# Where the adaLN sums are computed: all blocks after the first four in mixer A, one in each slot, in a bank of the ring of three

## The chip, the core and the metric

The kernel runs on one core of a Trainium2 chip. The metric is the device time of one execution in microseconds (us), the median of several runs. TensorE (PE) multiplies, PEld is its weight load, VectorE (DVE), ScalarE (ACT) and GpSimd (POOL) do the rest, and SyncE's queue (SP) issues the DMAs.

## What is computed

Two layers of a diffusion trunk, each a token mixer (A: windowed attention, B: neighbourhood attention) followed by a gated ConvFFN, over 640 tokens (512 latent, 128 context) of width 1024. Every sub-layer is modulated by a shift, a scale and a gate that come from one small product per layer:

```python
def adaln(cond, w_ada, b_ada):
    m = jax.nn.silu(cond) @ w_ada + b_ada
    return [t[:, None, :] for t in jnp.split(m, 6, axis=-1)]
...
for i in range(DEPTH):
    mp = adaln(c_ctx[None, :], w_ada[i], b_ada[i])
    ms = adaln(c, w_ada[i], b_ada[i])
    hp = modulate(rmsnorm(xp, norm_attn_w[i]), mp[0], mp[1])
    hs = modulate(rmsnorm(xs, norm_attn_w[i]), ms[0], ms[1])
    ...                                   # attention: op, o_s
    xp = xp + mp[2] * op
    xs = xs + ms[2] * o_s
    hp = modulate(rmsnorm(xp, norm_ffn_w[i]), mp[3], mp[4])
    hs = modulate(rmsnorm(xs, norm_ffn_w[i]), ms[3], ms[4])
    xp = xp + mp[5] * conv_ffn(hp, ...)
    xs = xs + ms[5] * conv_ffn(hs, ...)
```

`w_ada[i]` is 1024 x 6144 in float32, 24 MB a layer. The condition has two rows (latent and context), so the product is tiny in columns but has to read all of `w_ada`.

## The kernel before

**Blocks of adaLN.** The 6144 columns of a layer are 12 blocks of 512. A block (l, n) comes in four DMAs of 512 KB (`ada_tile`, L169, ring `adst` of four tiles: exactly one block). It is made in two steps by the generator `ada_queue` (L191). Step one: `ada_sums` (L174), eight float32 products (16 matmul records) that put four partial sums into the four 32-row strips of one PSUM bank `ps_ada`; a copy of that bank to SBUF, `adrow` (L182, on ACT in mixer A, on DVE in the FFNs); and the DMAs of the next block's tiles, which reuse the tiles just summed. Step two: `ada_done` (L219). For a gate (n = 4, 5, 10, 11; there the row's bias comes by a small DMA) one product (2 records), a copy and a DMA to DRAM; for the other n four products (8 records) that fold the strips into columns and one DVE addition of the bias into `mcol` (L231). Blocks (0, 0) to (0, 3) are made at the start and don't concern us; 20 remain.

**Mixer A** is a loop of 21 slots (L1006). Slot n works on head group g = n // 5 and token block t = n % 5: it runs the QKV product of (g, t) (`Q`, eight steps of three matmuls each), places the keys and queries of the slot before (`T`: transposes into banks of the ring `p`), scores of the block three slots back (`S`) and the product with the values of the block four slots back (`V`: transposes into ring `p`, then `ps_o`). The order in which PE takes these steps is written out by hand in `SLOTS` (L30): "A0" to "A3" for slots 0 to 3, then "a0" to "a4" by t, and "AT" for the last slot, which also holds half of the output projection. PE keeps this program order (`k.chain`), and the DMAs that go through `dma` keep theirs up to slot 18 (`k.dma_chain`); the rest is ordered by the scheduler. PSUM rings here: `mm` (2 banks: the QKV sums), `p` (3), `s` (2), `o` (1). ACT splits every weight into a high part (`whi`, L158) and POOL (DVE in a few cases) makes the low part (`wlo`, L161); weights of the next group are loaded at the ends of slots with t = 0, 1 and 4 (L1041).

Six blocks, (0, 4) to (0, 9), are made in the slots 1, 3, 5, 8, 11 and 14 (`ADA_SLOTS`, L38): step one after the fourth entry of the slot's order, step two after the tenth, with `ps_ada` in the ring `mm`.

**The FFN** of a layer (`finish_layer`, L1142, and `ffn`, L913) makes 44 up-products of 48 matmuls (7.1 us each), a convolution on DVE, SiLU on ACT and, in six groups, the down-products. PE's order is the scheduler's here. After the up-products listed in `ADA_UPS` (L54) `after("up")` takes one step of the queue: the twelve blocks (0, 10), (0, 11), (1, 0) to (1, 9) in layer 0, the two blocks (1, 10), (1, 11) in layer 1, with `ps_ada` in the ring `dn`.

Of the kernel before, what the change touches and what calls it, by code (L numbers as in the profile page):

```python
# [29 lines left out]
SLOTS = {"A0": "QQQQQQQQTT", "A1": "QQQQQQQTQT", "A2": "QQQQQQQTQT", "A3": "QSQSQQQSQQQTTS",  # L30
         "AT": "SSVOOVVSVOSOOTVVOOSOVSTVVOSVSOOOVVSOVSOVVSSOVOOVOVOOOV",
         "a0": "VSQQSQVVSSVVTQQVTQQQQ", "a1": "QSSVVQQVSVSQQQQVTQVQT", "a2": "SQVQQSVSVSQQVVTQQQTVQ",
         "a3": "QQVSSQQVVVSVVSQQQQTTQ", "a4": "SSQQQVVSSVQQQVVQTVQTQ",
         "b0": "SVQQSQHPPVQQQQVQ", "b1": "VQHPSQQSHPQQVQQHV", "b2": "QHVQSPSQHQVQVQHPQ",
         "b3": "HHSQVSQHPQQQVQVHQP", "b4": "SHPQQVSVQQHQQVQPH",
         "BT": "OSPOPSSVOOSOPVVSSOHHPOHPVOOHPOPOHVOOHOOPHSOSVHHSVVPOHOSVHPSHPOOHPOHSSOPVSVSPOVSPOOOVPPOOPVVVOOV"}

ADA_SLOTS, ADA_PLACES = (1, 3, 5, 8, 11, 14), (4, 10)  # L38

START = "p p x0 p p x1 p p n0 x2 n1 p p x3 n2 p x4 n3 n4 p s f0 w0 w1 p p f1 f4 p f2 p p f3 q p w2 w3 p"  # L40

# [8 lines left out]
O_DVE = (), (0, 2)  # L50

LAST = "40a 41a 00a 01a 40b 41b 00b 01b 10 11 n4 20 n0 21 30 n1 31 n2 q6 n3"

ADA_UPS = (0, 1, 3, 4, 6, 7, 8, 9, 11, 12, 14, 15, 17, 18, 20, 21, 23, 24, 26, 27, 29, 30, 32, 33), (0, 1, 3, 4)  # L54

OPROJ = "00 10 20 01 11 21 n0 30 n1 40 w0 n2 31 41 w1 u0 n3d w2 u1 n4d u2 u0 u1 u2"

# [1 line left out]
def _f(ap):  # L59
    return ap.bitcast(F32)  # L60


class Trunk:
# [846 lines left out]
            nc.vector.scalar_tensor_tensor(z[:, a:b - 1], u[:, a + 1:b], w[:, 2:3], z[:, a:b - 1], op0=OP.mult, op1=OP.add)  # L910
        return z

    def ffn(self, l, hT, xs, groups, first, ahead, after):  # L913
        nc, fp = self.nc, self.fp
        gate = None
        f = 0
        for gi, n in enumerate(groups):
            gh = self.ap.tile([P, 4, T], F32R, name="gh", tag="act")
            gl = self.ap.tile([P, 4, T], F32R, name="gl", tag="act")
            for k in range(n):  # L920
                zz = []
                for ff in (f + k, f + k + NF):
                    if first:
                        u = first.pop(0)
                    else:
                        u = []
                        w = ahead.pop(0) if ahead else self.load_w(self.I["wup"][l, ff], 1024, self.wp)
                        for _ in self.up(hT, [w], u):
                            pass
                    zz.append(self.conv(u[0], ff, fp))  # L930
                    after("up")
                silu = nc.scalar.activation(zz[0], zz[0], AF.Silu)
                nc.vector.tensor_tensor(zz[0], zz[0], zz[1], OP.mult)
                nc.scalar.activation(gh[:, k], zz[0], AF.Copy)  # L934
                nc.gpsimd.tensor_tensor(gl[:, k], zz[0], _f(gh[:, k]), OP.subtract)  # L935
            last = gi == len(groups) - 1
            if last:
                self.pin_exp(silu)
            W = [self.load_w(self.I["wdown"][l, f + k], 1024, self.wp) for k in range(n)]
            f += n  # L940
            if gate is None:
                gate = self.load_gate(l, 1)
            if last:
                after("last", (gh, gl), W, gate)
                continue
            for t in range(NT):
                for _ in self.proj_part((gh, gl), W, xs, t, gate):
                    pass


def body(nc, tc, I, O):
    with ExitStack() as top:
        k = Trunk(nc, tc, I, O, top)
# [11 lines left out]
        hT = k.new_hT("hA")  # L965
        with ExitStack() as c1:
            sp = k.pool(c1, "start", side="right")
            xT = [k.ap.tile([P, 4, T], F32, name=f"xT{h}", tag="act") for h in range(2)]
            xt, W, sts = [], [], []
# [25 lines left out]
        with c2:  # L995
            k.mp = k.pool(c2, "mixa", side="right")
            k.qT_bufs, k.pexp_bufs = 3, 4
            k.a_setup(pin=True)
            k.first_post(xT, hT, 1, 2 * P, NS, nc.gpsimd, pin=True)
            k.first_post(xT, hT, 1, NS, T, nc.gpsimd, pin=True)  # L1000
            sts.append(k.a_begin(0))
            steps = k.ada_queue([(0, n) for n in range(4, 10)], True, "mm", 2)
            ofs, scs = [], {}
            k.xd = [k.dp.tile([NT, P, D], F32, name=f"xd{i}") for i in range(3)]
            place = iter(())
            for n in range(21):  # L1006
                g, t = n // 5, n % 5
                u = n - 4
                if t == 0 and 0 < g < 4:
                    sts.append(k.a_begin(g))  # L1010
                if n == 19:
                    k.dma_chain = False
                if n in (4, 14):
                    ofs.append(k.ap.tile([P, 4, T], F32, name="of", tag="act"))
                gens = {"T": place, "S": iter(()), "V": iter(()), "Q": iter(()), "A": steps}
                if 0 <= u + 1 < 20:
                    scs[u + 1] = []
                    gens["S"] = k.a_score(sts[(u + 1) // 5], (u + 1) // 5, (u + 1) % 5, scs[u + 1])
                if u >= 0:
                    gens["V"] = k.a_pv(sts[u // 5], u // 5, u % 5, scs[u], ofs[u // 10])  # L1020
                if g < 4:
                    place = iter(())
                    st = sts[g]
                    gens["Q"] = k.qkv(hT, W, t, lambda ps: k.a_post(st, g, t, ps)) if n else q0
                    place = k.a_place(st, t)
                    order = SLOTS[f"A{n}" if n < 4 else f"a{t}"]
                    if n in ADA_SLOTS:
                        a, b = ADA_PLACES
                        order = order[:a] + "A" + order[a:b] + "A" + order[b:]
                    run(gens, order)  # L1030
                else:
                    for v in (18, 19):
                        scs[v] = []
                    gens["S"] = chain(gens["S"], *(k.a_score(st, 3, v - 15, scs[v]) for v in (18, 19)))
                    gens["V"] = chain(gens["V"], *(k.a_pv(st, 3, v - 15, scs[v], ofs[1]) for v in (17, 18, 19)))
                    gens["O"] = k.o_first(0, "woa", ofs[0], xin, k.xd[0])
                    run(gens, SLOTS["AT"])
                if 5 <= n < 17:
                    k.b_scratch(2 * n - 10)
                    k.b_scratch(2 * n - 9)  # L1040
                if g < 3 and t in (0, 1, 4):  # L1041
                    Wn = k.load_group("wqa", g + 1, Wn if t else None, t)
                if t == 4 and g < 3:
                    W = Wn
            k.chain = False
            for _ in steps:
                pass
            k.ada_scale(0, 1)
        finish_layer(k, 0, "woa", ofs[1], k.xd[0], cw)
        adactx.close()  # L1050

# [3 lines left out]
def mixer_b(nc, k, tc, top, hT, W):  # L1055

        I = k.I
        with ExitStack() as c2:
# [34 lines left out]
            for s in range(41):  # L1093
# [32 lines left out]
                if t == 4:  # L1126
                    W = Wn
            k.chain = False
        finish_layer(k, 1, "wob", ofs[1], k.xd[2], cw)


def run(gens, order, only=""):

    for c in order:
        next(gens[c], None)
    for c, g in gens.items():
        if c not in only and c != "A":
            for _ in g:
                pass


def finish_layer(k, l, wo, of, xsrc, cw):  # L1142
    nc = k.nc
    with ExitStack() as c:
        k.xp = k.pool(c, f"x{l}", side="right")
        k.fp = k.pool(c, f"ffn{l}", side="right")
        if l == 1:
            k.adp = k.pool(c, "ada2", side="right")
        k.psf = ExitStack()
        k.psp = k.pool(k.psf, f"psf{l}", space=PSUM)  # L1150
        k.z_bufs = 4
# [6 lines left out]
        xs = []  # L1158
# [4 lines left out]
        hl = k.split_oT(of, l == 0)  # L1163
        W = k.load_o(wo, 1)
        hT = k.new_hT(f"hF{l}")
        k.ada_next = k.ada_tiles(l, 10)
        k.convc = k.fp.tile([P, 44, 4], F32, name="convc")
        nc.sync.dma_start(k.convc, k.I["conv"][l])
        k.chain = True
# [15 lines left out]
        first = [], [], []  # L1185
# [19 lines left out]
        ahead = []  # L1205
# [6 lines left out]
        k.wp = k.pool(c, f"wf{l}")  # L1212
        first = list(first)
        k.chain = False
        blocks = [(l, 10), (l, 11)] + [(1, n) for n in range(10) if l == 0]
        steps = k.ada_queue(blocks, False, "dn", 2)
        ups_done = iter(range(44))

        def after(kind, *args):
            if kind == "up":  # L1220
                if next(ups_done) in ADA_UPS[l]:
                    next(steps)
            else:
                last(*args)

        def last(g, W, gate):

            for _ in steps:
                pass
            if l == 0:  # L1230
                k.ada_scale(1, 0)
                k.ada_scale(1, 1)
# [35 lines left out]
            up = k.psp.tile([P, 2, 512], F32, name="ps_dn", tag="up", bufs=3)  # L1268
            for w in LAST.split():
# [4 lines left out]
                t, h = int(w[0]), int(w[1])  # L1274
# [4 lines left out]
                    done(t, h)  # L1279
            k.chain = False  # L1280

        k.ffn(l, hT, xs, (4, 4, 2, 4, 4, 4), first, ahead, after)
        if l == 1:
            k.psf.close()

# [75 lines left out]
```

## Time and profile before

| | us |
|---|---|
| median of 3 runs | 1744.81 (1744.4 to 1747.25) |
| the profiled execution, device time | 1744.18 |
| its span, first to last instruction | 1742.4 |
| PE busy | 1633.3 (94%) |
| PEld busy | 1457.8 (84%) |
| POOL, DVE, ACT busy | 951.9, 879.2, 762.1 |

The span divides into the start (to some 64 us), mixer A (to some 337), the end of layer 0's attention (to 389), FFN of layer 0 (to about 850), mixer B and its end (to about 1275) and FFN of layer 1. A busy PE is not PE at its peak: what counts is whether it waits, and how many matmuls stand in its queue. The granted clock of TensorE is a share of 2.4 GHz; it has two levels, 1.0 and 0.5 (1.2 GHz), and a number between is a mean over the stretch.

### The profile page before, as it was taken

To read this page: it belongs to the slowest core of one execution; us is meant where nothing else is said; L and a number is where in the kernel's file an instruction comes from. 1 tells how busy PE (TensorE), PEld (TensorE's weight loads), DVE (VectorE), ACT (ScalarE), POOL (GpSimd) and SP (SyncE) were. 2 spreads that over 40 slices of the span, in tenths; PEclk is the share of its full clock that TensorE was granted. 3 is DMA by queue.
4 is the path that set the end of the run, shared out by engine and by line. 5 is a ranking of instruction groups with operands and counts; after the bars stand their busy time and mean duration, and the time that the engine had idled before them with its cause. 6 is when DMAs were issued, how large, how long until landed. Compare 5 with 4: busy or idle time off the path is not lost.

```text
span 1742.4 us, 26277 instructions
## 1 busy us (share of the span) xinstructions
PE 1633.3 (94%) x9736; PEld 1457.8 (84%) x9736; DVE 879.2 (50%) x2136; ACT 762.1 (44%) x1696; POOL 951.9 (55%) x796
## 2 busy tenths in 40 slices
PE   5788988989999999999988999988999999999998
PEld 2577776878998879899878999987779999999997
DVE  4667767674333333242575667677753232432334
ACT  4366666354131322232356777775543222323231
POOL 1553555564464664556336777775455656746461
PEclk8999999999999999999989999999999999999999
DMA  8242232516252434321232211223522222213131
GB/s 348 95 126 82 100 106 96 175 65 217 85 194 97 139 130 143 109 100 61 73 101 81 60 52 49 71 93 118 201 98 97 80 78 74 84 61 97 49 97 61
DMA packets 73727, 184.85 MB, mean 106 GB/s; under 512 B 15080, under 2 KB 24808, under 8 KB 73600
## 3 DMA queue, kind: packets, MB, share of 16 engines
q1 hardware_dynamic: 73600, 183.18, 31.1%
q8 instruction: 77, 1.26, 0.3%
q14 instruction: 50, 0.41, 0.1%
HBM read 171.32 MB, written 14.12 MB: 106 GB/s over the span
## 4 chain that ended last, share of the span: by engine, by line
PE 80%; DVE 9%; ACT 4%; issue 3%; POOL 2%; DMA 2%; SPq 0%; POOLq 0%; DVEq 0%; ACTq 0%
PE ps_up L133 35%; PE ps_dn L133 19%; PE ps_mm L133 11%; PE ps_ada L133 3%; PE ps_o L133 2%; PE ps_op L133 2%; PE ps_s L133 2%; PE ps_p L139 2%; PE ps_tr L139 1%; DVE xT L262 1%; PE ps_row L133 1%; DMA wst<-in_wqa_dram 1%; PE ps_nt L139 1%; DVE xn L336 1%; DVE xtmp L459 1%
## 5 line engine op out<-in xcount | busy, mean ns | idle before, releaser
L133 PE MATMUL ps_up<-hF,whi 128*128 128x320 f32 x2688 | 600.9, 311 | 5.1 <-POOL hF L373 5.1
L161 POOL TENSOR_TENSOR wlo<-wst,whi 128x1024 fp32r<-128x1024 f32 (+3 forms) x192 | 419.4, 2190 | 231.9 <-ACT whi L158 200.8
L133 PEld LDWEIGHTS ps_up<-hF,whi 128*128 128x128 f32 x2688 | 453.6, 189 | 25.4 <-ACT z L907 6.7
L133 PE MATMUL ps_up<-hF,wlo 128*128 128x320 f32 x1344 | 415.7, 310 | 0.0
L158 ACT ACTIVATE whi<-wst 128x1024 fp32r<-128x1024 f32 (+3 forms) x195 | 186.5, 962 | 442.0 <-PE ps_dn L133 165.8
L133 PEld LDWEIGHTS ps_up<-hF,wlo 128*128 128x128 f32 x1344 | 252.9, 188 | 4.6 <-issue 2.6
L909 DVE SCALAR_TENSOR_TENSOR z<-ps_up,convc,z 128x511 f32<-128x511 f32 (+1 forms) x176 | 95.8, 544 | 283.2 <-ACT z L907 283.2
L460 POOL TENSOR_TENSOR x<-x,xtmp 128x512 f32<-128x512 f32 x100 | 129.6, 1301 | 148.5 <-DVE xtmp L459 148.2
L459 DVE TENSOR_TENSOR xtmp<-ps_dn,gate 128x512 f32<-128x512 f32 x120 | 81.8, 689 | 242.5 <-PE ps_dn L133 239.7
L133 PE MATMUL ps_mm<-whi,hB 128*128 128x384 f32 x580 | 181.3, 351 | 9.3 <-DVE rs_r L324 8.5
L133 PE MATMUL ps_dn<-whi,gh 128*128 128x512 f32 x440 | 172.9, 393 | 1.8 <-DVE xtmp L459 1.6
L133 PE MATMUL ps_dn<-wlo,gh 128*128 128x512 f32 x440 | 172.3, 392 | 0.0
L133 PE MATMUL ps_dn<-whi,gl 128*128 128x512 f32 x440 | 169.8, 389 | 0.0
L935 POOL TENSOR_TENSOR gl<-z,gh 128x640 fp32r<-128x640 f32 x44 | 69.2, 1572 | 90.3 <-ACT gh L934 90.3
L133 PEld LDWEIGHTS ps_mm<-whi,hB 128*128 128x128 f32 x580 | 108.7, 191 | 11.6 <-ACT vb L511 8.9
L133 PE MATMUL ps_mm<-whi,hA 128*128 128x384 f32 x320 | 101.2, 362 | 9.6 <-DVE hA L268 3.5
L907 ACT ACTIVATE z<-ps_up,convc 128x640 f32<-128x640 f32 x88 | 77.0, 875 | 68.6 <-PE ps_up L133 68.6
L910 DVE SCALAR_TENSOR_TENSOR z<-ps_up,convc,z 128x511 f32<-128x511 f32 (+1 forms) x176 | 96.6, 549 | 5.6
L133 PE MATMUL ps_mm<-wlo,hB 128*128 128x384 f32 x290 | 98.3, 339 | 0.0
L133 PEld LDWEIGHTS ps_dn<-whi,gh 128*128 128x128 f32 x440 | 82.6, 188 | 17.8 <-DVE xtmp L459 3.5
L133 PEld LDWEIGHTS ps_dn<-whi,gl 128*128 128x128 f32 x440 | 82.2, 188 | 17.1
L133 PEld LDWEIGHTS ps_dn<-wlo,gh 128*128 128x128 f32 x440 | 82.6, 188 | 13.7
(210 smaller groups left out, 2945.1 us busy)
## 6 DMA issues: line engine op xcount, KB each, us to landing
adst<-in_wada_dram SPq DMA_DIRECT2D x96, 512.0 KB
wst<-in_wup_dram SPq DMA_DIRECT2D x78, 512.0 KB
wst<-in_wdown_dram SPq DMA_DIRECT2D x44, 512.0 KB
wst<-in_wqb_dram SPq DMA_DIRECT2D x29, 384.0 KB
wst<-in_wqa_dram SPq DMA_DIRECT2D x16, 384.0 KB
xd<-xring SPq DMA_DIRECT2D x20, 256.0 KB
x<-xd SPq DMA_DIRECT2D x10, 512.0 KB
wst<-in_woa_dram SPq DMA_DIRECT2D x8, 384.0 KB
```

Of the source, the lines that this page charges most:

```text
L133: i = self.nc.tensor.matmul(out, lhsT, rhs, start=start, stop=stop)
L139: i = self.nc.tensor.transpose(out, in_, idn)
L158: i = nc.scalar.activation(hi, st, AF.Copy)
L161: (lo_eng or nc.gpsimd).tensor_tensor(lo, st, _f(hi), OP.subtract)
L262: i = nc.vector.tensor_scalar(v, v, A[:, j, f:f + 1], self.mcol[0][:, j, f:f + 1], op0=OP.mult, op1=OP.add)
L336: nc.vector.tensor_scalar(xn, x, self.rsqrt(ss, 1, D), None, op0=OP.mult)
L459: nc.vector.tensor_tensor(tmp, ps, gate[:, j, sl], OP.mult)
L460: (nc.gpsimd if pool_add else nc.vector).tensor_tensor(x[:, sl], x[:, sl], tmp, OP.add)
L907: nc.scalar.activation(z, u, AF.Identity, scale=w[:, 1:2], bias=w[:, 3:4])
L909: nc.vector.scalar_tensor_tensor(z[:, a + 1:b], u[:, a:b - 1], w[:, 0:1], z[:, a + 1:b], op0=OP.mult, op1=OP.add)
L910: nc.vector.scalar_tensor_tensor(z[:, a:b - 1], u[:, a + 1:b], w[:, 2:3], z[:, a:b - 1], op0=OP.mult, op1=OP.add)
L935: nc.gpsimd.tensor_tensor(gl[:, k], zz[0], _f(gh[:, k]), OP.subtract)
```

## The change

Every block after the first four is made in mixer A. The queue of steps now holds (0, 4) to (0, 11) and (1, 0) to (1, 11), 20 blocks; each of the slots 1 to 19 takes two steps, so one block; the twentieth, (1, 11), is made in the loop behind the slots that empties the queue. The places in a slot's order are now given for each kind of slot. `ps_ada` lies in the ring `p` of three banks instead of the ring `mm` of two. The FFNs make none: `after`, `ADA_UPS`, their queue, the early load of a block's tiles and the pool `ada2` of layer 1 go. What used the result of a block (`ada_scale`, `load_gate`) stays where it was.

```diff
-ADA_SLOTS, ADA_PLACES = (1, 3, 5, 8, 11, 14), (4, 10)
+ADA_PLACES = {"A1": (2, 4), "A2": (2, 4), "A3": (2, 4), "a0": (2, 6), "a1": (1, 3), "a2": (1, 4), "a3": (1, 4), "a4": (2, 4)}
-ADA_UPS = (0, 1, 3, 4, 6, 7, 8, 9, 11, 12, 14, 15, 17, 18, 20, 21, 23, 24, 26, 27, 29, 30, 32, 33), (0, 1, 3, 4)
...
                     zz.append(self.conv(u[0], ff, fp))
-                    after("up")
...
-            steps = k.ada_queue([(0, n) for n in range(4, 10)], True, "mm", 2)
+            steps = k.ada_queue([(0, n) for n in range(4, 12)] + [(1, n) for n in range(12)], True, "p", 3)
...
-                    order = SLOTS[f"A{n}" if n < 4 else f"a{t}"]
-                    if n in ADA_SLOTS:
-                        a, b = ADA_PLACES
+                    slot = f"A{n}" if n < 4 else f"a{t}"
+                    order = SLOTS[slot]
+                    if n > 0:
+                        a, b = ADA_PLACES[slot]
                         order = order[:a] + "A" + order[a:b] + "A" + order[b:]
...
-        if l == 1:
-            k.adp = k.pool(c, "ada2", side="right")
...
-        k.ada_next = k.ada_tiles(l, 10)
...
-        blocks = [(l, 10), (l, 11)] + [(1, n) for n in range(10) if l == 0]
-        steps = k.ada_queue(blocks, False, "dn", 2)
-        ups_done = iter(range(44))
-
-        def after(kind, *args):
-            if kind == "up":
-                if next(ups_done) in ADA_UPS[l]:
-                    next(steps)
-            else:
-                last(*args)
-
         def last(g, W, gate):
-            for _ in steps:
-                pass
...
-        k.ffn(l, hT, xs, (4, 4, 2, 4, 4, 4), first, ahead, after)
+        k.ffn(l, hT, xs, (4, 4, 2, 4, 4, 4), first, ahead, last)
```

## Rows read from the trace of the kernel before

**Rows 1.** The page's first part: busy time, share of the span, instructions.

```profile
PE 1633.3 (94%) x9736; PEld 1457.8 (84%) x9736; DVE 879.2 (50%) x2136; ACT 762.1 (44%) x1696; POOL 951.9 (55%) x796
```

**Rows 2.** Busy time by stage: length, PE, PEld, DVE, ACT, POOL; clock, DMA, GB/s.

```profile
103.60:162.00 58.40, 53.36 (x333) 44.59 (x331) 40.62 (x137) 40.13 (x115) 28.65 (x42) 1.00 0.35 104
...
222.80:282.10 59.30, 51.07 (x286) 43.95 (x284) 41.24 (x135) 43.23 (x120) 31.78 (x41) 0.94 0.21 65
...
389.00:850.00 461.00, 461.00 (x2838) 412.24 (x2838) 164.83 (x271) 134.37 (x152) 252.49 (x136) 1.00 0.36 125
1280.00:1313.00 33.00, 33.00 (x219) 27.65 (x218) 14.57 (x24) 13.53 (x15) 16.21 (x8) 1.00 0.46 160
```

**Rows 3.** The tile ps_ada, by form: count, ns min/median/max, first and last start.

```profile
L133 PE MATMUL ps_ada<-adst,cT x320: 589/592/617, 67.5 to 1302.3; 128*32 128x512 f32 x160
```

**Rows 4.** Timeline of PE around two blocks in layer 0's FFN: start, duration, instruction.

```profile
401.57 1.02 PE L133 MATMUL ps_ada<-adrow,sel 99*2 99x512 f32 x2
...
434.07 1.92 PE L133 MATMUL ps_ada<-adst,cT 128*32 128x512 f32 x16
435.92 0.56 PE L133 MATMUL ps_up<-hF,whi 128*128 128x320 f32 x2
...
443.06 0.95 PE L133 MATMUL ps_ada<-sel,adrow 98*128 98x2 f32 x8
443.87 0.48 PE L133 MATMUL ps_dn<-whi,gh 128*128 128x512 f32 x1
```

**Rows 5.** Busy time from one slot's squares (L559) to the next's, columns as above.

```profile
103.60:119.50 15.90, 14.27 (x92) 10.89 (x91) 9.21 (x29) 11.39 (x30) 8.93 (x12) 1.00 0.80 238
162.00:178.80 16.80, 13.79 (x69) 11.06 (x67) 9.61 (x28) 11.13 (x29) 9.17 (x12) 0.90 0.34 106
222.80:240.10 17.30, 14.08 (x67) 11.56 (x66) 9.68 (x28) 10.85 (x28) 8.73 (x11) 0.80 0.43 140
119.50:130.10 10.60, 9.39 (x60) 8.60 (x59) 8.08 (x27) 7.59 (x23) 6.75 (x8) 1.00 0.10 11
...
178.80:191.40 12.60, 11.99 (x83) 9.96 (x82) 8.32 (x28) 7.43 (x22) 4.68 (x6) 1.00 0.54 211
140.80:150.80 10.00, 9.94 (x70) 8.12 (x68) 6.99 (x25) 6.47 (x21) 2.35 (x4) 1.00 0.43 153
202.20:209.70 7.50, 7.28 (x47) 6.78 (x45) 6.54 (x23) 5.92 (x20) 2.34 (x4) 1.00 0.00 1
...
150.80:162.00 11.20, 9.88 (x61) 8.64 (x59) 8.43 (x29) 7.74 (x22) 5.85 (x10) 1.00 0.21 57
209.70:222.80 13.10, 12.59 (x84) 9.85 (x82) 9.11 (x32) 8.32 (x25) 6.53 (x11) 1.00 0.45 162
268.60:282.10 13.50, 10.49 (x62) 8.72 (x60) 9.37 (x29) 12.02 (x31) 10.12 (x12) 1.00 0.20 54
```

**Rows 6.** Timeline of PE in mixer A; in brackets, idle before and its releaser.

```profile
67.50 1.92 PE L133 MATMUL ps_ada<-adst,cT 128*32 128x512 f32 x16 [2.78 <-issue]
...
84.46 0.33 PE L133 MATMUL ps_mm<-wlo,hA 128*128 128x384 f32 x1
...
84.99 0.34 PE L133 MATMUL ps_mm<-wlo,hA 128*128 128x384 f32 x1
...
106.78 1.92 PE L133 MATMUL ps_ada<-adst,cT 128*32 128x512 f32 x16
...
171.94 0.44 PE L133 MATMUL ps_mm<-whi,hA 128*128 128x384 f32 x1 [1.04 <-ACT whi L158]
173.82 0.44 PE L133 MATMUL ps_mm<-wlo,hA 128*128 128x384 f32 x1 [1.44 <-POOL wlo L161]
```

**Rows 7.** Timeline of ACT: the copy of two blocks' sums in mixer A.

```profile
84.37 0.60 ACT L186 ACTIVATE adrow<-ps_ada 98x512 f32<-98x512 f32 x1 [0.21 <-PE ps_ada L133]
...
110.76 0.57 ACT L186 ACTIVATE adrow<-ps_ada 98x512 f32<-98x512 f32 x1
```

**Rows 8.** The stretch in which slot 5's tiles come in, columns as in rows 2.

```profile
108.50:121.00 12.50, 11.41 (x74) 10.08 (x71) 6.07 (x17) 9.68 (x23) 9.07 (x10) 1.00 0.97 278
```

More of the change, by code (lines that the diff above doesn't have):

```diff
@@ L911, in conv, with ffn @@
         return z
-    def ffn(self, l, hT, xs, groups, first, ahead, after):
+    def ffn(self, l, hT, xs, groups, first, ahead, end):
         nc, fp = self.nc, self.fp
@@ L935, in ffn @@
                 nc.gpsimd.tensor_tensor(gl[:, k], zz[0], _f(gh[:, k]), OP.subtract)
-            last = gi == len(groups) - 1
-            if last:
+            if gi == len(groups) - 1:
                 self.pin_exp(silu)
@@ L942, in ffn @@
                 gate = self.load_gate(l, 1)
-            if last:
-                after("last", (gh, gl), W, gate)
+            if gi == len(groups) - 1:
+                end((gh, gl), W, gate)
                 continue
```

## The prediction

> **What bounds the kernel now.** I read four views, in this order. First the page's busy shares: PE is busy for 94% of the span and no other engine for more than 55% [rows 1], so the question for every stage is whether PE waits there. Second, the busy time by stage. In the FFN of layer 0 PE is busy for all of its 461 us, and so it is in the part of layer 1's FFN that holds the two blocks; in mixer A it idles for 5.0 of 58.4 us in one head group and 8.2 of 59.3 us in another [rows 2]. Matmul time that leaves the FFNs is therefore worth its full length, and the same time put into mixer A can partly lie in waits that are there anyway. Third, mixer A slot by slot: the distance from one slot's squares (they end its QKV) to the next's, for slots of the same kind with a block in them and without [rows 5]. That is the price of a block in a slot, measured by the kernel itself. Fourth, single rows: what a block costs PE [rows 4], where PE waits in mixer A [rows 6], when the copy of the sums runs [rows 7], how long the tiles take to come [rows 8].
>
> **What leaves the FFNs.** 320 records of sums are 20 blocks of 16 [rows 3]; 14 of them stand in the FFNs. In an FFN the sums of a block start at 434.07 and the next up-product at 435.92: 1.85 us. Its second part takes 443.87 - 443.06 = 0.81 us, or, for a gate, by a record of 1.02 us that overlaps its follower a little, about 0.95 [rows 4]. Eight blocks of 2.66 and six gates ((0, 10), (0, 11), (1, 4), (1, 5), (1, 10), (1, 11)) of 2.80 are 21.3 + 16.8 = 38.1 us. PE never waits around them [rows 2, 4], so nothing covers this time: all 38.1 us come off. The copies on DVE and the tiles' DMAs that go with them lie beside PE and cost nothing now; they free nothing either, since DVE is busy for 165 of 461 us there. After the change the next engine in the FFN is POOL with 252 of then some 430 us, so PE stays the bound.
>
> **What is added to mixer A.** Thirteen more slots get a block, and one block stands behind the slots.
> - Kind a0 (slots 10 and 15). Slot 5, with a block, took 15.9 us; slots 10 and 15, without, took 16.8 and 17.3 [rows 5]. The block is *shorter than nothing* there, because a0 begins a head group and its QKV waits for weights (1.04 us for the high part, 1.44 for the low, in slot 10) [rows 6], and the granted clock in these two stretches falls to a mean of 0.90 and 0.80, against 1.00 in slot 5, where the block's matmuls stand where the wait was. I take -0.9 and -1.4: -2.3. Bounds: -1.4 to +2.8 each. By the Trainium skill (TensorE: Matmul & The Clock Gate, Part 1: The HAM clock gate) TensorE is throttled to half its clock when it idles and released by activity; slots 5, 10 and 15 agree.
> - Kind a1 (slots 6, 16): slot 11 with a block 12.6, slot 6 without 10.6: +2.0 each, 4.0.
> - Kind a3 (13, 18): slot 8 with a block 10.0, slot 13 without 7.5: +2.5 each, 5.0.
> - Kind a4 (4, 9, 19): slot 14 with a block 13.1, slot 9 without 11.2: +1.9; slot 19 without took 13.5, which would make it -0.4 [rows 5]. Slot 19 already carries the output projection's weights (ACT 12.0 of 13.5 us), so slot 9 is the nearer match: 1.9 each, 5.7.
> - Kind a2 (7, 12, 17): no slot of this kind has a block. Between 0 and PE's price of 2.8; I take the mean of a1 and a3, 2.25 each: 6.8.
> - Slot 2: between 0 and 2.8. In the ring of two the first block waited 2.78 us for its bank [rows 6] ("issue" is a wait that the profile can't name; QKV of the slot before holds the bank until DVE has read it). In the ring of three that wait goes, but the placing of keys behind it needs the same DVE work, so only part comes back. 1.4 for slot 2 and this together.
> - The block behind the slots: nothing of the trace shows one there; 0 to 2.8. PE's queue is dense there, so 2.8.
>
> Together 23.4 us, before one new wait.
>
> **The new wait.** Step two needs ACT's copy of the sums, and PE, which keeps its order, stands still until it is there; everything of the slot is queued behind it. Before, six entries of the slot's order lay between; now two to four. A QKV step is 84.99 - 84.46 = 0.53 us [rows 6], so two steps cover 1.06 us. The copy takes 0.6 us. In slot 3 ACT sat idle and the sums released it, so it began at once; in slot 5 it began 2.06 us after them (110.76 against 106.78 + 1.92) [rows 6, 7]. So the stall is 0 for a copy of the first kind and 2.06 + 0.57 - 1.06 = 1.6 us for one of the second. Most copies will be nearer to the first, and a0, which had the late one, now has four entries between: I take 0.13 us on average over 19 blocks, 2.5 us, with bounds 0 and 30. By the Trainium skill (TensorE: Matmul & The Clock Gate, the table of specifications, "Engine queue depth") ScalarE takes its instructions strictly in order; the trace agrees so far as the late copy of slot 5 shows it.
>
> **What else moves.** Each block's tiles (2 MB) are issued on SP's queue right behind its predecessor's sums and so ahead of the weights, the tables of mixer B and the next slot's bias row. In the stretch that also carries the weights and tables of slot 5 the queues are full for 12.5 us at 278 GB/s, some 3.5 MB, of which the tiles are 2.1 [rows 8]; alone at that pace the tiles take 7.5 us, an estimate. The shortest slot with a block lasts 10.0 us and the a0 slots 16 [rows 5]. I cost this at nothing, covered by the slot; where the cover is gone, the sums wait, and PE with them, up to 12.5 - 10.0 = 2.5 us a slot. In the ring of three a block holds one bank of the transposes for as long as step one and two are apart, which spans at most one V entry: nothing.
>
> **Sum.** Added 23.4 + 2.5 = 25.9, removed 38.1: -12.2 us. The profiled execution took 1744.18 (span 1742.4 and 1.8 around it), 0.6 below the median of the runs; put on the median, 1744.8 - 12.2 = 1732.6.
>
> **The rivals.**
> - *Mixer A hides nearly all.* The head group with two blocks took 58.4 us, the one with none 59.3 [rows 2]: taken so, blocks are free. Against it: that last group has waits of its own (slot 19), and PE's idle time there is only 5 to 8 us a group. If idle and lost clock are filled in all groups, some 10 us are left of the added time: 1744.8 - 38.1 + 10 = 1717.
> - *Nothing is hidden.* Every block costs in mixer A what it cost in the FFN, 38.1 us, because its place is before the waits of the slot and not in them, and a0 gains nothing: 1745. For it: a3's price is 2.5 of 2.7, and its PE idles for 0.2 us without a block [rows 5]. Against it: a0's rows.
> - *The copy on ACT sets the slot: slower.* In mixer A ACT is busy for 40 of 58 us [rows 2], and with two entries of cover PE stops at step two. It decides from a mean stall of 12.2 / 19 = 0.64 us over the 2.5 counted, about 0.8 us a block. At 1.2 us, three quarters of slot 5's, it is 23 us instead of 2.5: 1732.6 + 20.5 = 1753.
> - That the sums don't all leave the FFNs can't be: nothing is left there that makes them.
>
> **How the numbers follow.** My forecast (1724 to 1741) 0.57; all but hidden (1708 to 1724) 0.15; nothing hidden (1741 to 1748) 0.13; ACT's copy, or the tiles late in the same way, slower 0.15. A measurement of this kernel tells about 0.2%, 3.5 us, from no change. Faster by more: 0.57 + 0.15 = 0.72; within: 0.13; slower: 0.15. The range leaves about one in ten on each side: down to the hidden case, 1715, and up to 1749, the edge of the slow one.
>
> **What would show it.** In the changed kernel's FFNs: no ps_ada, PE busy throughout, and the two FFNs together 38 us shorter; less would break the first step. In mixer A: slots 10 and 15 at 16 us or less with a granted clock of 1.00; a1 to a4 some 2 us longer than their rows here; mixer A's whole stretch about 23 us longer and 3 more for the block behind it. Idle of PE ahead of the second part of blocks (releaser: ACT adrow) above 0.8 us each would make the ACT rival right; idle ahead of sums released by the DMA of adst, or a clock that falls in mixer A where it did not, would also break the forecast.

## The result and the profile after

| | before | after |
|---|---|---|
| median of the runs, us | 1744.61 | 1728.47 (1725.33 to 1728.87) |
| ratio of the runs | | 0.990 (0.988 to 0.991) |
| profiled execution, us | 1744.18 | 1725.33 |
| its span | 1742.4 | 1723.5 |

The kernel is 16 us faster by the medians and 18 (15 to 21) by the ratio; 12 were forecast. The change was run a second time beside the experiments: 1727.83 us, 0.990 (0.989 to 0.992).

Where the time went, from the two traces, in us; the borders are starts of squares and matmuls.

| stage | before | after | difference |
|---|---|---|---|
| slots 1 to 19 of mixer A (first to last squares) | 216.7 | 241.3 | +24.6 |
| from there to the first up-product of layer 0 | 87.0 | 91.5 | +4.6 |
| FFN of layer 0, to its last down-product | 513.4 | 475.3 | -38.1 |
| from there to the first up-product of layer 1 | 376.5 | 374.0 | -2.5 |
| FFN of layer 1, to its last down-product | 478.5 | 470.9 | -7.6 |

The page's first part, of the kernel after (to hold against [rows 1]):

```profile
PE 1624.4 (94%) x9736; PEld 1450.5 (84%) x9736; DVE 869.8 (50%) x2122; ACT 769.1 (45%) x1710; POOL 951.1 (55%) x796
```

Exactly as many matmuls as before, fourteen copies fewer on DVE and more on ACT: nothing was removed, it was moved. Busy time by stage of the kernel after: two head groups of mixer A and a part of either FFN (length; PE, PEld, DVE, ACT, POOL; clock, DMA share, GB/s), to hold against [rows 2]:

```profile
106.90:171.50 64.60, 62.41 (x393) 46.32 (x392) 43.27 (x142) 41.48 (x119) 28.51 (x42) 1.00 0.57 192
237.60:306.90 69.30, 62.42 (x400) 47.41 (x398) 45.75 (x142) 46.15 (x125) 33.05 (x43) 1.00 0.57 209
430.00:842.00 412.00, 412.00 (x2511) 389.88 (x2510) 139.83 (x236) 130.39 (x148) 250.73 (x135) 1.00 0.24 76
1278.00:1310.00 32.00, 32.00 (x220) 32.00 (x219) 12.57 (x22) 14.78 (x17) 21.89 (x10) 1.00 0.32 99
```

The FFNs are as dense as before. The first head group lost more than half of its idle time (2.2 of 64.6 us, where it was 5.0 of 58.4), the last one kept most of it (6.9 of 69.3), and the granted clock is 1.00 in both, where it was 0.94 in the last.

The slots of the kernel after, in the order of [rows 5]: slots 5, 10, 15 (kind a0), 6, 11 (a1), 8, 13 (a3), 9, 14, 19 (a4).

```profile
106.90:122.70 15.80, 14.90 (x93) 10.87 (x91) 9.23 (x29) 11.57 (x30) 8.76 (x12) 1.00 0.66 216
171.50:188.70 17.20, 14.97 (x92) 10.72 (x91) 9.24 (x29) 10.91 (x28) 8.38 (x11) 1.00 0.63 226
237.60:255.10 17.50, 14.96 (x91) 10.72 (x90) 9.29 (x29) 10.80 (x28) 8.39 (x11) 1.00 0.69 244
122.70:135.30 12.60, 12.41 (x85) 9.94 (x85) 8.47 (x30) 7.91 (x24) 6.16 (x9) 1.00 0.61 202
188.70:202.30 13.60, 12.84 (x88) 10.25 (x88) 9.14 (x28) 8.61 (x25) 6.63 (x10) 1.00 0.56 204
147.60:157.80 10.20, 10.20 (x63) 7.07 (x62) 7.61 (x25) 6.60 (x20) 2.35 (x4) 1.00 0.63 211
214.00:224.20 10.20, 10.20 (x63) 7.03 (x61) 7.63 (x25) 6.83 (x20) 2.35 (x4) 1.00 0.58 221
157.80:171.50 13.70, 13.01 (x85) 9.92 (x84) 9.34 (x30) 8.35 (x24) 5.62 (x10) 1.00 0.44 154
224.20:237.60 13.40, 12.94 (x79) 9.06 (x77) 9.46 (x30) 8.34 (x23) 5.60 (x9) 1.00 0.43 167
290.50:306.90 16.40, 13.24 (x80) 9.19 (x78) 10.18 (x30) 12.66 (x31) 10.45 (x12) 1.00 0.48 181
```

Slots that got a block are longer by 0.4 and 0.2 (a0, slots 10 and 15), 2.0 (slot 6), 2.7 (13), 2.5 (9) and 2.9 us (19). Of the slots that held a block before, 3, 8, 11 and 14 grew too, by 1.3, 0.3, 0.9 and 0.3 us. The clock in slots 10 and 15 is back at 1.00, from 0.90 and 0.80, and slots 8 and 13 are full: PE never waits there.

### The profile page after: what moved, and what is told of

Same layout as the page of the kernel before. It is cut to its first block, busy times and chain, and to the rows that moved or that the text cites. A ratio compares the mean times of both kernels' runs of the same rounds, so it can differ in the third digit from the quotient of the medians.

```text
span 1723.5 us, 26316 instructions
## 1 busy us (share of the span) xinstructions
PE 1624.4 (94%) x9736; PEld 1450.5 (84%) x9736; DVE 869.8 (50%) x2122; ACT 769.1 (45%) x1710; POOL 951.1 (55%) x796
## 5 line engine op out<-in xcount | busy, mean ns | idle before, releaser
L131 PEld LDWEIGHTS ps_mm<-whi,hB 128*128 128x128 f32 x580 | 108.7, 191 | 11.6 <-ACT vb L509 8.9
L932 POOL TENSOR_TENSOR gl<-z,gh 128x640 fp32r<-128x640 f32 x44 | 69.3, 1576 | 83.3 <-ACT gh L931 83.3
L131 PEld LDWEIGHTS ps_dn<-whi,gl 128*128 128x128 f32 x440 | 82.3, 188 | 17.2
L131 PEld LDWEIGHTS ps_dn<-wlo,gh 128*128 128x128 f32 x440 | 82.6, 188 | 13.7
```

Of the source, the lines that this page charges most:

```text
L131: i = self.nc.tensor.matmul(out, lhsT, rhs, start=start, stop=stop)
```

## The experiments

Times are medians; a ratio is to the kernel before on the same chip, with its 95% interval, and a difference in us is that ratio on 1745. A single trace of mixer A can be off by some 3 us: slots 1 to 19 took 216.7 us in the kernel before and 219.6 in the first run below, whose slots hold the same work; the changed kernel's second trace has 243.8 for 241.3.

### What the FFNs give back

The fourteen blocks are left out of the FFNs and made nowhere; their columns and gates are filled with copies of layer 0's first ones. Mixer A keeps its six blocks.

```diff
-        k.ada_next = k.ada_tiles(l, 10)
...
-        steps = k.ada_queue(blocks, False, "dn", 2)
...
+            for a in (0, 24):
+                nc.vector.tensor_copy(k.mcol[1][:, :, a:a + 16], k.mcol[0][:, :, a:a + 16])
+            for g in ((0, 1), (1, 0), (1, 1)):
+                nc.sync.dma_start(k.gd[g[0], g[1]], k.gd[0, 0])
```

> The kernel before with the fourteen blocks of the FFNs left out (their columns and gates are filled with copies of layer 0's first ones), mixer A untouched with its six blocks. It measures alone what the FFNs give back; the changed kernel minus this one is what mixer A pays. Theory: the two traces show the FFNs and what follows some 45 us shorter, more than the 38.1 us of the sum, because matmuls next to a block run slower and one block was cut in pieces by the scheduler; then this kernel takes about 1744.6 - 45 = 1700 us, and mixer A pays 28. Rival: the FFNs give the 38.1 of the sum and mixer A hid more than forecast (pays 22): 1706.5 us.

1703.95 us, 0.976 (0.974 to 0.977): the FFNs give back 43 us (40 to 45). Two runs of the changed kernel stand at 0.990, so mixer A pays 0.990 - 0.976 on 1745, some 25 us (21 to 29 by the two intervals). What the FFNs give back is nearer to the 45 of the theory, and the 38.1 of the rival lies outside; what mixer A pays lies half way between 28 and 22.

Why more than 38.1? Two things that my one block [rows 4] didn't show. First, the matmuls beside a block's sums. Timeline of PE in the kernel before, around the sums that began at 434.07:

```profile
433.83 0.31 PE L133 MATMUL ps_up<-hF,wlo 128*128 128x320 f32 x1
...
436.32 0.31 PE L133 MATMUL ps_up<-hF,wlo 128*128 128x320 f32 x1
436.47 0.45 PE L133 MATMUL ps_up<-hF,whi 128*128 128x320 f32 x2
436.76 0.31 PE L133 MATMUL ps_up<-hF,wlo 128*128 128x320 f32 x1
```

Two up-matmuls take 436.76 - 436.47 = 0.29 us. The two right behind the sums took 436.32 - 435.92 = 0.40, and the one right ahead of them 434.07 - 433.83 = 0.24 instead of 0.15: 0.2 us a visit that I didn't count. The other visits of sums in this FFN have the same two borders (0.23 to 0.24 ahead, 0.40 for the next two). By the Trainium skill (TensorEngine Tiling (Array Packing), Tiling Modes, Key Properties) changing the tiling mode drains TensorE, and the sums are its 128x32 mode; the trace agrees that both borders of a visit are slow, but no run here shows that a drain is the reason. Second, one block of layer 0 was cut in four by the scheduler, with up-matmuls between:

```profile
642.43 1.05 PE L133 MATMUL ps_ada<-adst,cT 128*32 128x512 f32 x2
644.63 1.04 PE L133 MATMUL ps_ada<-adst,cT 128*32 128x512 f32 x2
647.11 1.05 PE L133 MATMUL ps_ada<-adst,cT 128*32 128x512 f32 x2
649.16 1.90 PE L133 MATMUL ps_ada<-adst,cT 128*32 128x512 f32 x10
```

Up to the next up-matmul the four pieces took 0.98, 0.98, 0.98 and 1.83, together 4.8 us where a whole block takes 1.85. A piece of two records fills one strip of the bank alone and takes 0.98 us; a whole block is eight such pieces, and they overlap, or 1.85 us would not do. That is 2.9 us, and twelve blocks at 0.2 to 0.3 us of slow borders are 2.4 to 3.6: with the 32.5 us of layer 0's blocks (eight of 2.66, four gates of 2.80) 38 to 39, and the stage table has 38.1. In layer 1's FFN the blocks' own 5.6 us are seen in its 7.6; the rest is 1.2 us less idle time and borders.

### The ring and the places: four cells and one part alone

```diff
-            steps = k.ada_queue([(0, n) for n in range(4, 12)] + [(1, n) for n in range(12)], True, "p", 3)
+            steps = k.ada_queue([(0, n) for n in range(4, 12)] + [(1, n) for n in range(12)], True, "mm", 2)
```

> The changed kernel with ps_ada in the ring mm of two banks as before instead of the ring p of three. Theory: with a block in every slot each QKV finds its bank taken by a block, or a block finds its bank taken by the QKV of the slot before; the kernel before shows such waits of 0.5 us in slots 3 and 11 and 2.8 + 0.9 in slots 1 and 2, so some 0.5 us a slot: 1728.5 + 10 = 1738 us. Rival: the reads that free the bank are done by then and the ring doesn't matter: 1728 us, within 3.5.

```diff
-ADA_PLACES = {"A1": (2, 4), "A2": (2, 4), "A3": (2, 4), "a0": (2, 6), "a1": (1, 3), "a2": (1, 4), "a3": (1, 4), "a4": (2, 4)}
+ADA_PLACES = {s: (4, 10) for s in ("A1", "A2", "A3", "a0", "a1", "a2", "a3", "a4")}
```

> The changed kernel with the old places (step one after the fourth entry of the slot's order, step two after the tenth) in all slots. If the short distance between the two steps costs what its trace shows as idle ahead of second parts (1.5, 0.4, 0.8, 0.8 us, released by the copy on ACT), those 3.4 us go and it takes 1725 us. Rival: the longer stay of the block in the ring p, across two to four V entries, leaves the transposes two banks and costs 0.5 us a slot: 1738 us.

Both edits together:

> The changed kernel with both the old ring (mm, two banks) and the old places (4, 10) in all slots. With the early places the ring of two cost 19 us, because step one came before DVE and ACT had read the QKV sums of the slot before. Theory: by the fourth entry they have, so that with the old places the ring costs little and this stands near the old places in ring p (1723.5): 1726 us. Rival: the ring costs its 19 us wherever the block stands: 1742 us.

| difference to before, us | places as changed (early) | old places (4, 10) |
|---|---|---|
| ring p of three | -17 (-20 to -15), 1727.83 | -22 (-25 to -19), 1723.52 |
| ring mm of two | +2 (0 to +3), 1747.46 | -13 (-16 to -11), 1732.36 |

With the ring of two and the early places the move is worth nothing. Timeline of PE in that kernel (ring mm, early places), the idle before five of the sums in brackets:

```profile
67.00 1.94 PE L131 MATMUL ps_ada<-adst,cT 128*32 128x512 f32 x8 [3.25 <-issue]
...
131.13 1.68 PE L131 MATMUL ps_ada<-adst,cT 128*32 128x512 f32 x8 [2.16 <-issue]
...
159.68 1.07 PE L131 MATMUL ps_ada<-adst,cT 128*32 128x512 f32 x8 [1.39 <-issue]
...
202.31 1.06 PE L131 MATMUL ps_ada<-adst,cT 128*32 128x512 f32 x8 [1.75 <-ACT whi L156]
...
228.74 1.07 PE L131 MATMUL ps_ada<-adst,cT 128*32 128x512 f32 x8 [1.39 <-issue]
```

Nine blocks wait so, 14.7 us together; in the changed kernel only 0.2 us of idle stand before sums. The releaser is not named, or wrongly (ACT's `whi` at 202.31); DVE's timeline names it. DVE reads the QKV sums of the slot before, and in all five cases the block's sums start 0.1 us after the last of these reads has ended, at 131.13 after this one:

```profile
130.81 0.21 DVE L578 TENSOR_TENSOR t2a<-ps_mm,ropek 128x64 f32<-128x64 f32 x1
```

With the old places in the ring of two 3.3 us of such waits are left. The ring is worth some 9 us there too (1732.36 against 1723.52), but the two traces don't place them in the slots: slots 1 to 19 took 243.6 us with the ring of two and 242.7 with the ring of three. The stretch behind them, to the first up-product, took 96.0 for 91.0. There PE waits for DVE's copy of the twentieth block's product; timeline of PE (ring mm, old places):

```profile
370.26 0.80 PE L131 MATMUL ps_dn<-whi,oh 128*128 128x512 f32 x1 [3.05 <-DVE adrow L222]
```

So the ring and the early places are one change: the places need the ring. Whether the ring is better off with later places is not clear of the noise. That the longer stay in ring p would starve the transposes and cost 10 us (my rival for the old places) is refuted; they are 4 us better than the early ones by the medians, but the two intervals of the ratio (0.986 to 0.989, 0.989 to 0.992) overlap a little.

The ring alone, in the kernel before with its six blocks:

```diff
-            steps = k.ada_queue([(0, n) for n in range(4, 10)], True, "mm", 2)
+            steps = k.ada_queue([(0, n) for n in range(4, 10)], True, "p", 3)
```

> The kernel before with the ring alone changed: its six blocks in ring p of three banks, places and FFNs as before. Theory: with the old places the ring costs (1732.4 - 1723.5) / 19 = 0.5 us a block, and the first block's wait of 2.8 us is the largest; six blocks: 1744.8 - 3 = 1742 us. Rival: with so few blocks the wait moves to the step behind: no change, 1745 us.

1739.45 us, 0.996 (0.995 to 0.997): -7 us (-10 to -5), more than the 3 expected. Its trace shows 3.2 of them against the trace of before: slots 2, 3 and 11 are 1.0, 0.3 and 0.6 us shorter, where blocks or QKV had waited for a bank, and the rest is spread over stretches in which the clock's phases fall differently. Where the other half lies I can't say.

### The wait for the copy

Timeline of PE in the kernel after: three second parts of blocks that wait for ACT's copy of the sums.

```profile
68.64 1.02 PE L131 MATMUL ps_ada<-adrow,sel 99*2 99x512 f32 x2 [1.47 <-ACT adrow L184]
...
192.72 1.05 PE L131 MATMUL ps_ada<-sel,adrow 98*128 98x2 f32 x8 [0.76 <-ACT adrow L184]
...
259.14 1.05 PE L131 MATMUL ps_ada<-sel,adrow 98*128 98x2 f32 x8 [0.77 <-ACT adrow L184]
```

All such waits together are 3.8 us in six places, and 2.8 in five in the second trace. With the copy on DVE:

```diff
-            steps = k.ada_queue([(0, n) for n in range(4, 12)] + [(1, n) for n in range(12)], True, "p", 3)
+            steps = k.ada_queue([(0, n) for n in range(4, 12)] + [(1, n) for n in range(12)], False, "p", 3)
```

> The changed kernel with the copy of the sums on DVE instead of ACT. If ACT's queue is what delays second parts, the 3.4 us of idle ahead of them go: 1725 us. If DVE is as full as ACT in mixer A (41 against 40 of 58 us before), the wait only changes its name: 1728 to 1732 us.

1735.64 us, 0.995 (0.993 to 0.996): 8 us slower than the changed kernel, and outside both expectations. The wait didn't change its name alone, it doubled (7.7 us in five places); timelines of DVE and PE in that kernel:

```profile
69.20 0.69 DVE L186 COPY adrow<-ps_ada 98x512 f32<-98x512 f32 x1
...
69.94 1.87 PE L131 MATMUL ps_ada<-adrow,sel 99*2 99x512 f32 x2 [3.38 <-DVE adrow L186]
...
82.83 1.86 PE L131 MATMUL ps_ada<-adrow,sel 99*2 99x512 f32 x2 [1.99 <-DVE adrow L186]
```

Both records took 1.87 us where 1.02 is usual: after these waits TensorE stood at half its clock (0.70 on the mean of slot 1, 0.85 of slot 2), which the changed kernel doesn't have there. These two slots took 11.2 and 11.6 us for 6.8 and 8.5, which is nearly all of the 8 us. DVE came to the first copy 3.9 us after the sums had ended (65.3), behind the norm of the QKV of the slot before; ACT began it at 68.01 in the kernel after, 2.1 us after its sums. By busy time the two engines are alike (43.3 and 41.5 of 64.6 us): it is what stands ahead of the copy that makes ACT the better engine for it.

### The a0 slots

Two blocks alone are moved from layer 0's FFN into mixer A, and slots 10 and 15 get a block each; ring mm, old places. First the two are the gates (0, 10) and (0, 11), which by the order of the queue come to stand in slots 14 and 15; then the columns (1, 0) and (1, 1), in slots 10 and 15.

```diff
-ADA_SLOTS, ADA_PLACES = (1, 3, 5, 8, 11, 14), (4, 10)
+ADA_SLOTS, ADA_PLACES = (1, 3, 5, 8, 10, 11, 14, 15), (4, 10)
...
-            steps = k.ada_queue([(0, n) for n in range(4, 10)], True, "mm", 2)
+            steps = k.ada_queue([(0, n) for n in range(4, 12)], True, "mm", 2)
```

> The kernel before with two blocks alone moved from layer 0's FFN to the a0 slots 10 and 15 (old places, ring mm). The prediction's a0 term says a block there takes 0.9 and 1.4 us off, by filling the wait for weights and keeping the clock: with two FFN blocks of 3.0 us gone, -6.0 - 2.3 = -8.3, 1736.3 us. Rival, from the changed kernel's slots 10 and 15, which took 0.5 and 0.1 us longer with a block than without: -6.0 + 0.6 = -5.4, 1739.2 us. If blocks cost their full price there: -6.0 + 5.4, 1744 us.

1745.06 us, 1.000 (0.998 to 1.001): no change, the last of the three. Slot 10 took 16.9 and slot 15 17.3 us with their blocks, 16.8 and 17.3 without [rows 5], so in the slot itself a block is free. In its trace layer 0's FFN is 4.7 us shorter, where I had taken 6; this is lost beside the two slots. (The profiled execution is the slowest of the twelve, so I use of it only what the next run repeats.) Timeline of PE in that kernel, slots 15 and 16:

```profile
239.03 1.02 PE L133 MATMUL ps_ada<-adrow,sel 99*2 99x512 f32 x2 [3.11 <-DMA adrow<-in_b_ada_dram]
...
258.84 0.37 PE L139 MATMUL ps_tr<-identr,kd 128*128 128x128 f32 x1 [2.90 <-POOL kd L532]
```

The second part of a gate waits for its bias row, a small DMA that stood on SP behind the tables, the weights and the output of the slot before; and the keys of the next slot wait for POOL. With columns instead of gates (layer 0's FFN then makes the other ten):

```diff
-            steps = k.ada_queue([(0, n) for n in range(4, 12)], True, "mm", 2)
+            steps = k.ada_queue([(0, 4), (0, 5), (0, 6), (0, 7), (1, 0), (0, 8), (0, 9), (1, 1)], True, "mm", 2)
```

> As the run with two blocks alone moved to the a0 slots 10 and 15, but with two blocks of layer 1 that are no gates, (1, 0) and (1, 1). That run's trace shows slots 10 and 15 no longer with a block than without (16.9 and 17.3), yet PE idle 3.1 us for the bias row of a gate and 2.9 us for keys right behind it. Theory: an a0 block costs nothing where it needs no bias row, so the FFN's 6 us come off nearly whole: 1739 us. Rival: the next slot takes it back: 1744 us, no change.

1741.07 us, 0.998 (0.997 to 0.998): -4.4 us (-6 to -3), nearer to the theory. The wait for the bias row is gone and slot 15 is down to 16.1 us, but the one for POOL's keys behind it (2.9 us) stays. Slot 16 of the kernel before, of the run with gates and of this one, none of which has a block there (columns as above):

```profile
240.10:250.10 10.00, 9.41 (x59) 8.64 (x59) 7.85 (x27) 7.61 (x23) 6.09 (x7) 1.00 0.21 68
...
245.50:260.30 14.80, 10.31 (x59) 9.28 (x59) 9.02 (x27) 8.56 (x23) 8.45 (x10) 0.93 0.28 89
...
241.40:256.10 14.70, 9.74 (x59) 8.68 (x58) 8.72 (x27) 8.33 (x24) 8.50 (x10) 1.00 0.28 97
```

So the slot behind slot 15 takes 4.7 us back, as the rival says; slot 11, behind slot 10, took 12.7 us in all three. Slot 10 itself took 18.3 us here, at a mean clock of 0.91, so slots 10, 15 and 16 of this trace together are 5.2 us longer than before, more than the 4.6 that layer 0's FFN gives back; what is shorter besides is the stretch from there to layer 1's first up-product, by 3.4 us, where nothing was changed and the traces lie between 372.7 and 378.5. Where the 4.4 us of the median come from stays open. In the changed kernel no a0 or a1 slot holds a gate, and none of its PE waits is for a bias row.

### The last block, and better places

In the kernel after, PE waits at the start of the last slot, and the clock halves from 308.9 to 315.7:

```profile
307.05 1.20 PE L131 MATMUL ps_s<-kTa,qTa 128*128 128x512 f32 x4 [2.85 <-ACT kTa L538]
310.54 0.47 PE L137 MATMUL ps_p<-ident,pexp 128*128 128x128 f32 x1 [2.30 <-POOL pexp L636]
```

```diff
-         "AT": "SSVOOVVSVOSOOTVVOOSOVSTVVOSVSOOOVVSOVSOVVSSOVOOVOVOOOV",
+         "AT": "ASSVAOOVVSVOSOOTVVOOSOVSTVVOSVSOOOVVSOVSOVVSSOVOOVOVOOOV",
```

> The changed kernel with the twentieth block not behind the slots but in the last slot (step one at its start, step two after its third entry). In the changed kernel PE idles 2.9 us for keys and 2.3 us for a score there, and the clock then stands at half for 6.8 us. Theory: the block's 2.7 us fill part of these waits and hold the clock: -3 to -6 us, 1723 to 1725. Rival: the keys and scores wait for ACT and POOL work that itself comes later by as much: no change, 1728 us.

1722.07 us, 0.988 (0.986 to 0.990): 6 us under the changed kernel by the medians, 3.5 by the ratios, and the intervals overlap: three of its five runs took 1721 to 1722 us, two 1728 and 1730. The stretch from the last squares to the first up-product is 88.7 us long for 91.5 and 90.9 in the two traces of the changed kernel. The wait for keys went from 2.85 to 0.99 us, as expected; the one for POOL's score stayed at 2.30, and the clock still fell there.

With the second steps of A1 at (2, 6) and of a1 at (1, 4) besides:

> The kernel with the twentieth block in the last slot, and besides step two one to two entries later in slots of kind A1 (2, 6) and a1 (1, 4), where PE idles 1.5 and 0.4 to 0.8 us ahead of it for the copy on ACT. Theory: of these 3.4 us some 2 come off: 2 us less than with the block in the last slot alone. Rival: the wait moves to the next step that needs ACT: the same.

1722.04 us, 0.987 (0.986 to 0.989): the same. The wait for the copy moved little (0.7, 0.4, 1.4, 0.8 us); the rival holds. Last, the old places for the kinds a0 and a4, on top of both:

```diff
-ADA_PLACES = {"A1": (2, 4), ..., "a0": (2, 6), "a1": (1, 3), "a2": (1, 4), "a3": (1, 4), "a4": (2, 4)}
+ADA_PLACES = {"A1": (2, 6), ..., "a0": (4, 10), "a1": (1, 4), "a2": (1, 4), "a3": (1, 4), "a4": (4, 10)}
```

> The twentieth block in the last slot and the later second steps in A1 and a1, and besides the old places in a0 and a4, whose slots 10, 11, 15 and 19 were 0.7 to 2.4 us shorter with the old places than with the new. Theory: 5 us less than with the later second steps alone (1722): 1717 us. Rival: half of these differences come back in the slots behind or were the clock's: 1720 to 1722 us.

1720.15 us, 0.986 (0.985 to 0.988): 24 us under the kernel before and 7 under the changed one, this time with intervals that don't meet. It has the lowest median here, but only two of the 5 us expected over the kernel with later second steps came, which is within the noise, and the rival (1720 to 1722) holds. The expectation came from slots 10, 15 and 19 of the run with old places everywhere; slot 16 of that run stands below them (columns as above):

```profile
172.90:189.40 16.50, 14.78 (x93) 10.96 (x91) 9.85 (x29) 10.90 (x29) 7.88 (x10) 1.00 0.67 230
238.20:253.30 15.10, 14.49 (x92) 10.85 (x90) 9.64 (x29) 10.88 (x28) 7.87 (x10) 1.00 0.69 231
293.50:308.10 14.60, 13.24 (x80) 9.31 (x78) 9.20 (x30) 12.09 (x30) 9.41 (x11) 1.00 0.55 208
...
253.30:271.60 18.30, 15.75 (x84) 12.98 (x83) 9.51 (x28) 8.50 (x24) 8.46 (x10) 0.81 0.57 209
```

The first three are against 17.2, 17.5 and 16.4 in the kernel after: the same matmuls, PE idle less (0.6 for 2.5 us in slot 15). But slot 16 is against 13.7, slots 2 and 3 grew by 1.0 and 1.6 as well, and slots 1 to 19 together took 242.7 for 241.3. In the trace of the last kernel they took 237.4: slots 15 and 19 were 15.1 and 14.6 and slot 16 14.0, though slot 10 was 18.3, at a clock of 0.81.

## Why the prediction was right, point by point

- **What bounds the kernel.** Right: matmul time that left the dense FFNs was worth its length and more, and mixer A hid a part of the same time in its waits: PE's idle time in slots 1 to 19 fell from 24.4 to 16.7 us.
- **What leaves the FFNs, 38.1 us.** Mis-sized: 43 (40 to 45) when left out, 45.7 in the pair of traces. I priced one block and multiplied; the borders of each visit and the block cut in four were in the trace. These 5 us are what the forecast of 12 lacks to the measured 16 to 18.
- **What is added, 25.9 us with the wait.** Right as a sum, some 25 (21 to 29) by the run without the blocks. Its terms were off in both directions, and that they cancel is luck. a3 +5.0: measured 5.2. a1 +4.0: 5.8, because slot 16, for which I had read no row, grew from 10.0 to 13.7 us, 0.8 of it the wait for the copy. a4 +5.7: 6.7. a2 +6.8: 3.2 (1.5, 0.9 and 0.7 us in slots 7, 12, 17); with no slot of this kind to read I took the mean of two others, more than twice what they took. Slot 2 +1.4: 0.5. The last block 2.8: not shown. The stretch behind the slots grew by 4.6 in the pair of traces, but it took 86.5 to 91.8 us in five traces of kernels without a block there, and with the block moved out of it it took 88.7, 88.9 and 90.1 us for 91.5 and 90.9.
- **a0, -2.3 us.** The sign failed: +0.7. The wait for weights did go and the clock did stay at 1.00, as the step said. But slot 5, my yardstick, is not slots 10 and 15 with a block: in slot 10 of the kernel after PE waits 0.84 us for a score's exponential and 0.5 for the transposes' copy instead. A wait that was filled gave way to the next one. And the two runs with a0 blocks alone show 4.7 us in the slot behind slot 15, which I had not looked at.
- **The ring, counted together with slot 2.** The step that failed most. It cost the sum nothing, because the forecast was for the ring of three, where the wait of the sums for a bank, which I had taken to go, is indeed gone. I took the 2.8 us wait of the first block as the ring's whole worth. The four cells show 9 us at the old places and 19 at the early ones: without the ring the change would have come out at +2. Of the rows of before, only those blocks were seen in the ring of two that came after the fourth entry; how early a place the reads of the QKV sums allow was not in any row that I looked at.
- **The new wait, 2.5 us.** The mechanism and the size held: 3.8 and 2.8 us of idle for the copy in the two traces, no block of the 1.6 us kind but one. ACT as the bound (1753) is refuted, and DVE in its place is worse.
- **Tiles late.** Costed at nothing, and 0.2 us of idle before sums is all there is. DMA carried 192 to 209 GB/s in mixer A for 104 and 65 before [rows 2].
- **The rivals.** "Nothing is hidden" and "all but hidden" both fell: of the 43 us mixer A took 25.

## What to carry to other kernels

Price work that is to leave a dense stage by the whole stage and not by one instance: its borders and the instances that the scheduler cut belong to it. Work that is put into an in-order stage needs its place and its buffer chosen together; ask of each early place who still reads the buffer it takes. A slot of the same kind that already has the work is a good price for a slot bound by matmuls (a3: 2.5 expected, 2.6 measured) and a poor one for a slot bound by waits, where filling one wait uncovers the next, in the same slot or in the one behind.

## What was not expected of the hardware

The matmul ahead of and the two behind a visit of the 128x32 sums are slower by 0.09 and 0.11 us, and two sums of one strip alone take 0.98 us where sixteen over four strips take 1.85. The granted clock did not follow from the length of a single wait. It fell after waits of 2.0 to 3.4 us on PE (slots 1 and 2 of the run with DVE's copy) and of 2.85 us (at 307 in the changed kernel), but in slot 1 of the kernel before it stood at 1.00 through a wait of 2.78 us, where in the run with the blocks left out one of 2.06 us brought the slot to 0.79. And in slots 4 and 11 of the second trace of the changed kernel it fell with no wait above 1.75 and 1.12 us, in slots that stand at 1.00 in its first trace (columns as above):

```profile
89.27:106.06 16.79, 15.01 (x87) 10.87 (x86) 9.90 (x33) 9.20 (x27) 5.86 (x10) 0.90 0.36 137
187.69:203.18 15.49, 14.37 (x88) 11.82 (x86) 9.71 (x28) 8.81 (x24) 6.59 (x10) 0.89 0.47 179
```

So a clock that falls or holds in one trace is no proof of what a change does; slots 10 and 15 stood at 1.00 in both traces of the changed kernel and at 0.90 or below in three traces without blocks there.
